# Splitting the second group's operands step by step, and moving the finish of reloaded blocks into the v stage

## The chip, the cores and the metric

The kernel runs on one core of a Trainium2 chip. The metric is device time in microseconds (us). The kernel before takes 2644.31 us, the median of three runs between 2639.09 and 2648.97. A core has five engines that matter here: TensorE (PE, matmuls), VectorE (DVE), ScalarE (ACT), GpSimd (POOL), and SyncE (SP). Each runs its own instructions in order. In this kernel SP's DMA queue carries the weights, and POOL's queue carries the activations, spills and results.

## The reference

One layer of a decoder, for a prompt of 2048 tokens and a sample batch of 8 x 8 tokens, in float32:

```python
z = rms_norm(x, pre_g)
xr, gr, u, v, gs = split(z @ w_in)            # 5 x 1024 columns
xc, new_buf = causal_depthwise_conv(xr, conv_buf, conv_w, conv_b)
r, i = sigmoid(xc . w_r + b_r), sigmoid(xc . w_i + b_i)     # per head
a = exp(-8 r softplus(-lam));  h_t = a_t h_{t-1} + sqrt(1 - a_t^2) i_t xc_t
br = h * silu(gr)
v = rms_norm(gelu(v), sgu_g)
bs = gelu(u) * (tril(w_s) @ v per chunk of 128 + b_s) * silu(gs)
y = x + rms_norm(concat([br, bs]) @ w_out, post_g)
```

The outputs are y for prompt and sample, the last three rows of the convolution, the last h, and the sample's normalised v.

## The kernel before

The prompt is cut into four groups of 512 tokens. Group 0 also carries the 64 sample tokens. Every large product is made of three matmuls on rounded halves: a float32 matrix is split into a high part (hi, made by ACT) and the rest (lo, made by DVE), and hi x hi, hi x lo and lo x hi are added in PSUM. Weights come as 128 x 1024 blocks of 512 KB by SP's queue (`wraw`, L176). ACT makes `wh` (L184), DVE makes `wl` (L192). The pools hold three of each.

Group 0 uses ordinary products (`gm0...`, L363), laid out by a scheduler. Its jobs end with 16 `out` jobs. In these also the beginning of group 1 is done: `stat_load` loads x in a token-major form (`xs`, L613), `stat_sum` squares and sums it on ACT (L621), `stat_rstd` makes the inverse root mean square and spreads it on a diagonal (`xd`, L630, DVE), `stat_spread` multiplies with ones on PE (`nsx`, L635), `stat_take` copies it back (L639). `z_raw` loads x in the form for the products (`xr`, L643), `z_norm` normalises it (L649, DVE).

Groups 1 to 3 use a Strassen-like scheme of seven products (`PROD` = B11, P4, B21, P2, P1, P3, B22) with the operands A11, A22, A12, E, D1, D3, F (`ACTS`). `pre` (L666 to L672, DVE) forms E, D1, D3 and F in place of the blocks of A, `z_hi` (ACT, L678) and `z_lo` (DVE, L683) split them into the tiles R1A, R1E, R1D, R1F that PE reads. (The trace merges A11, A22, A12 under R1A, and D1, D3 under R1D.) These groups run under a schedule by hand: `steps2` is a list of weight blocks with their matmuls, and `at2(step, f, ...)` hangs a piece of other work on a step. Within a step each engine executes: the loads of weights 6 steps ahead, `wh` 3 steps ahead, the hung work, `wl` 3 steps ahead, then the matmuls. So an instruction that waits on ACT or DVE holds up the weight halves of the following steps.

One group has 196 steps. From its first step G: four quads `xg0` to `xg3` of 14 steps (columns xr and gr); the v stage of 28 steps from V = G + 56; four quads `ug` from U = G + 84; and two wide stages of the output product, 28 steps each, from O = G + 140. The convolution, the gates and the scan of a quad (ACT lines L855 to L870, DVE lines L874 to L885) hang on the steps behind it. The end of the v stage's first product, `vn` (ACT, L789, gelu from PSUM) and its squares (`vq`, L910), stands about 12 steps into that stage.

The finish of a group's result y = x + rms_norm(out) needs the sum of squares over all columns, so it is done in the next group. Group 0's 16 blocks of 288 KB are spilled to DRAM and reloaded (`finish0_load`, L595), scaled on DVE (`finish0_scale`, L599), x is added by an accumulating DMA (`finish0_add`, L602), and the result stored (`finish0_store`, L605). Of the later groups' eight blocks of 512 KB, four stay in SBUF and four are spilled and reloaded (`finish_load`, L994); then `finish_scale` (L1000, twice per block), `finish_add` (L1004) and `finish_store` (L1007). `load_gq` (L983) loads a piece of the post-norm gain. All these DMAs but gq are issued on POOL.

Nearly all large tiles (xr, gr, gates, r, i, q, t, vn, u, the reloaded blocks fo, gq, xs) are taken in turn from one pool of 13 buffers of 128 x 2 x 516 floats:

```python
dp = ctx.enter_context(tc.tile_pool(name="dp", bufs=13))
```

A new tile waits until the buffer's last user is through. Where that is a DMA, the instruction waits for its landing. Tiles are assigned to buffers in the order in which the program asks for them.

Of the kernel before, what the change touches and what calls it, by code (L numbers as in the profile page):

```python
# [51 lines left out]
def hybrid_layer(ctx: ExitStack, tc: tile.TileContext, a):  # L52
# [683 lines left out]
    def at2(s, f, *args):  # L736

        tasks[s].append((f, *args))
# [337 lines left out]
    def at(job, f, *args):  # L1076
        plan[job].append((f, *args))
# [26 lines left out]
        t = 60 + 20.5 * n  # L1104
        by_step[next(i for i, x in enumerate(when) if x >= t)].append((make_sums, u))
    for n in range(8):
        at(("out", 8 + n // 4), stat_load, 1, n)
        at(("out", 9 + n // 4), stat_sum, 1, n)
    for f in (stat_rstd, stat_spread, stat_take):
        at(("out", 11), f, 1)  # L1110
    for j in range(8):
        at(("out", 10 + j // 2), z_raw, 1, j)
        at(("out", 12 + j // 3), z_norm, 1, j)

    z_load(0)
    make_identity(nc, ident)
# [30 lines left out]
    zlo = ctx.enter_context(tc.tile_pool(name="zlo", bufs=4, reuse_waits="tile"))  # L1147
    zhi = ctx.enter_context(tc.tile_pool(name="zhi", bufs=4, reuse_waits="tile"))

    for c in ACTS:  # L1150
        for j in range(4):
            if c == "E":
                pre(("R", 1), "D3", j)
            if c in ("E", "D1", "F"):
                pre(("R", 1), c, j)
            z_hi(("R", 1), c, j)
            z_lo(("R", 1), c, j)

    def combine(key, c, j, s):

        at2(s, z_hi, key, c, j)
        at2(s + 1, z_lo, key, c, j)

    for g in range(1, NG):
        G = len(steps2)
        V, U, O, R2 = G + 56, G + 84, G + 140, G + 168
        for n, us in enumerate(XG):
            quad(g, f"xg{n}", us, put_xg(g, 2 * n))  # L1170
            e, k = len(steps2), (g, 2 * n)
            at2(e - 8, gate_weights, *k)
            at2(e - 3, gate_weights_split, *k)
            at2(e, conv_first, *k, 0)
            at2(e + 1, conv_first, *k, 1)
            for m in range(6):
                at2(e + 1 + m // 2, conv_tap, *k, m // 3, 1 + m % 3)
            at2(e + 4, gate_hi, *k)
            at2(e + 5, gate_lo, *k)
            at2(e + 6, act, ("gr", *k), AF.Silu)  # L1180
            late[e + 6].append((gate_mm, *k, 0))
            at2(e + 7, gate_sig, *k, 0)
            late[e + 8].append((gate_mm, *k, 1))
            at2(e + 9, gate_sig, *k, 1)
            at2(e + 10, lru_tanh, *k)
            ts = (11, 11, 12, 13, 14, 18, 20, 21, 22) if n < 3 else (10, 11, 11, 12, 13, 14, 15, 16, 17)
            for t, (f, *args) in zip(ts, ((mul, ("i", *k), ("xc", *k)), (lru_exp, *k), (lru_sq, *k), (lru_mult, *k),
                                          (act, ("t", *k), AF.Sqrt), (mul, ("i", *k), ("t", *k)),
                                          (lru_scan, *k, 0), (lru_scan, *k, 1), (lru_end, *k))):
                at2(e + t, f, *args)  # L1190
        wide(g, "v", "w_v", 0, put_v(g))
        if g == 1:
            for j in range(KT):
                t = 4 + 3 * j // 2 if j < 10 else V + 11 + 2 * (j - 10)
                at2(t, finish0_load, j)
                t = max(t + 3, 9)
                at2(t, finish0_scale, j)
                at2(t + 1, finish0_add, j)
                at2(t + 4, finish0_store, j)
        else:  # L1200
            at2(G - 1, load_gq, g - 1, 1)
            for n in range(4):
                k = (g - 1, (1, 1, 0, 0)[n], (3, 2, 2, 3)[n])
                at2(G + 4 + n, finish_scale, *k)
                at2(G + 5 + n, finish_add, *k)
                at2(G + 10 + n, finish_store, *k)
            at2(G + 8, load_gq, g - 1, 0)
            for n in range(4):
                k = (g - 1, n % 2, n // 2)
                at2(G + 5 + n, finish_load, *k)  # L1210
                at2(G + 11 + n, finish_scale, *k)
                at2(G + 12 + n, finish_add, *k)
                at2(G + 17 + n, finish_store, *k)
        at2(U + 2, norm_v, g)
        at2(U + 3, scale_v, g, 0)
        at2(U + 5, scale_v, g, 1)
        for n, us in enumerate(UG):
            quad(g, f"ug{n}", us, put_ug(g, 2 * n))
            e, k = len(steps2), (g, 2 * n)
            for i in range(2):  # L1220
                late[e - 10 + 2 * i].append((spatial_prod, *k, i))
                at2(e - 9 + 2 * i, spatial_take, *k, i)
            at2(e + 1, act, ("u", *k), AF.Gelu_apprx_tanh)
            at2(e + 2, mul, ("u", *k), ("s", *k))
            at2(e + 3, act, ("gs", *k), AF.Silu)
            at2(e + 4, end_u, *k)
        B, key = O - 14, ("C", g)
        for j in range(4):
            combine(key, "A11", j, B + 3 + j)
            combine(key, "A22", j, (B + 7, B + 7, B + 8, O + 5)[j])  # L1230
            at2((B + 8, B + 10, B + 12, O + 2)[j], pre, key, "D3", j)
            combine(key, "A12", j, (B + 9, B + 11, B + 12, O + 6)[j])
            s = (B + 10, B + 13, O + 1, O + 7)[j]
            at2(s, pre, key, "E", j)
            combine(key, "E", j, s + 1)
            at2(O + 8 + j, pre, key, "D1", j)
            combine(key, "D1", j, O + 9 + j)
            combine(key, "D3", j, O + 13 + j)
            at2(O + 17 + j, pre, key, "F", j)
            combine(key, "F", j, O + 18 + j)  # L1240
        for q in range(2):
            wide(g, f"o{q}", "w_or", q, put_o(g, q))
        at2(len(steps2) + 2, out_rstd, g)
        if g + 1 < NG:
            for n in range(8):
                at2(O + 2 + 3 * n // 2, stat_load, g + 1, n)
                at2(O + 5 + 3 * n // 2, stat_sum, g + 1, n)
            at2(O + 18, stat_rstd, g + 1)
            late[O + 19].append((stat_spread, g + 1))
            at2(O + 20, stat_take, g + 1)  # L1250
            for j in range(8):
                at2(O + 18 + j, z_raw, g + 1, j)
                for i in range(2):
                    at2(O + 22 + 2 * j + i, z_norm, g + 1, j, (i,))
            key = ("R", g + 1)
            for j in range(4):
                combine(key, "A11", j, R2 + 2 + j)
                combine(key, "A22", j, R2 + 8 + j)
                at2(R2 + 10 + j, pre, key, "D3", j)
                combine(key, "A12", j, R2 + 12 + j)  # L1260
                at2(R2 + 14 + j, pre, key, "E", j)
                combine(key, "E", j, R2 + 16 + j)
                at2(R2 + 18 + j, pre, key, "D1", j)
                combine(key, "D1", j, R2 + 19 + j)
                combine(key, "D3", j, R2 + 23 + j)
                at2(R2 + 21 + j, pre, key, "F", j)
                combine(key, "F", j, R2 + 26 + j)
# [97 lines left out]
```

## Time and profile before

| what | value |
|---|---|
| median of 3 runs | 2644.31 us (2639.09 to 2648.97) |
| the profiled execution, its own time | 2642.0 us |
| its span in the trace | 2640.0 us |
| mean granted TensorE clock | 0.981 of full speed |
| PE busy | 2523.5 us (96%) |
| DVE busy | 1767.9 us (67%) |
| ACT busy | 1390.9 us (53%) |
| POOL busy | 339.9 us (13%) |
| bytes by SP's queue | 383.36 MB |
| bytes by POOL's queue | 201.11 MB |

The span of a quad (14 steps) without disturbance is 43.1 us in this trace, that of a v stage 83.2 to 86.2 us. A row of waits gives who waited, at which line, for which engine and tile, then the sum of us, the number of waits and the longest. A row of groups gives line, engine, operation, tiles and shapes, then busy time, mean ns of one, and the idle time ahead of it with what ended it. In a row of DMA issues the last number is the median us from issue to landing. The granted clock is that of PE, 1.00 being full speed.

### The profile page before, as it was taken

The numbers are of one execution on the slowest core, as the hardware profiler recorded it, in microseconds if no ns is written. First come the engines' busy times: TensorE is split into PE (matmuls) and PEld (weight loads), VectorE is DVE, ScalarE is ACT, GpSimd is POOL, SyncE is SP. The second block draws the span as 40 slices with busy tenths as digits, with TensorE's granted clock in tenths as the row PEclk, the third lists the DMA queues.
The fourth block names the chain that finished last, engine by engine and source line by source line (L and its number), as shares of the span: only waits on it lengthen the run. The fifth ranks groups of instructions, "written<-read, shape, count | busy, mean of one in ns | idle before, by whom it ended". The sixth has DMA issues, their size and how long they took to land.

```text
span 2640.0 us, 41631 instructions
## 1 busy us (share of the span) xinstructions
PE 2523.5 (96%) x16710; PEld 2321.1 (88%) x16710; DVE 1767.9 (67%) x2293; ACT 1390.9 (53%) x1778; POOL 339.9 (13%) x492
## 2 busy tenths in 40 slices
PE   7999999899998999999999999999999899999994
PEld 6999789899988998899878898899878898899883
DVE  7885255545457687656888586656788686666855
ACT  5445331123234577645766577645765577555642
POOL 4332023323331200100100200000100200000000
PEclk9999999999998999999999999999999999999997
DMA  6994378865864855756876955556776965555555
GB/s 224 342 342 174 118 262 307 313 247 196 315 235 151 280 183 178 239 180 182 266 260 210 299 192 163 184 180 189 269 238 216 297 191 165 184 183 177 185 190 191
DMA packets 168802, 587.12 MB, mean 222 GB/s; under 512 B 19344, under 2 KB 19904, under 8 KB 168608
## 3 DMA queue, kind: packets, MB, share of 16 engines
q1 hardware_dynamic: 110064, 383.36, 44.3%
q0 software_dynamic: 58544, 201.11, 22.4%
q8 instruction: 130, 2.13, 0.3%
q14 instruction: 64, 0.52, 0.1%
HBM read 494.92 MB, written 89.47 MB: 221 GB/s over the span
## 4 chain that ended last, share of the span: by engine, by line
PE 72%; DMA 10%; DVE 7%; ACT 6%; issue 4%; POOL 1%; SPq 0%; DVEq 0%; ACTq 0%; POOLq 0%
PE gm0out L363 6%; PE gm0v L374 4%; PE gm0gr L363 4%; PE gm0gs L363 3%; PE gm0xr L363 2%; DMA wraw_c_P<-P_c 1%; DMA pB22c<-w_in 1%; PE gm0u L363 1%; PE g L849 1%; PE sp L552 1%; PE w3vd L709 1%; DVE wl_c_B L192 1%; PE w2o1a L709 1%; PE w1o1a L709 1%; PE w2o0a L709 1%
## 5 line engine op out<-in xcount | busy, mean ns | idle before, releaser
L184 ACT ACTIVATE wh_c_P<-wraw_c_P 128x1024 fp32r<-128x1024 f32 x192 | 203.2, 1059 | 277.0 <-DMA wraw_c_P<-P_c 69.3
L192 DVE TENSOR_TENSOR wl_c_P<-wraw_c_P,wh_c_P 128x1024 fp32r<-128x1024 f32 x192 | 234.7, 1223 | 113.4 <-ACT wh_c_P L184 111.5
L192 DVE TENSOR_TENSOR wl_c_B<-wraw_c_B,wh_c_B 128x1024 fp32r<-128x1024 f32 x144 | 175.5, 1222 | 86.9 <-ACT wh_c_B L184 86.8
L184 ACT ACTIVATE wh_c_B<-wraw_c_B 128x1024 fp32r<-128x1024 f32 x144 | 151.9, 1056 | 140.2 <-DMA wraw_c_B<-w_in 44.1
L192 DVE TENSOR_TENSOR wl_w_or_P<-wraw_w_or_P,wh_w_or_P 128x1024 fp32r<-128x1024 f32 x96 | 117.5, 1223 | 50.1 <-ACT wh_w_or_P L184 49.7
L184 ACT ACTIVATE wh_w_or_P<-wraw_w_or_P 128x1024 fp32r<-128x1024 f32 x96 | 101.5, 1057 | 84.6 <-DMA wraw_w_or_P<-P_w_or 20.8
L184 ACT ACTIVATE wh_w_or_B<-wraw_w_or_B 128x1024 fp32r<-128x1024 f32 x72 | 76.1, 1058 | 79.6 <-DMA wraw_w_or_B<-w_or 18.4
L363 PE MATMUL gm0out<-c0l,wh_out 128*128 128x288 f32 x512 | 111.9, 300 | 1.2 <-DVE c0l L158 1.1
L363 PE MATMUL gm0out<-c0h,wh_out 128*128 128x288 f32 x512 | 110.4, 297 | 0.9 <-ACT wh_out L184 0.9
L192 DVE TENSOR_TENSOR wl_w_or_B<-wraw_w_or_B,wh_w_or_B 128x1024 fp32r<-128x1024 f32 x72 | 88.0, 1222 | 34.6 <-ACT wh_w_or_B L184 34.3
L363 PE MATMUL gm0out<-c0h,wl_out 128*128 128x288 f32 x512 | 110.2, 297 | 0.5 <-DVE wl_out L192 0.5
L363 PEld LDWEIGHTS gm0out<-c0l,wh_out 128*128 128x128 f32 x512 | 83.1, 190 | 2.6 <-DVE c0l L158 1.9
L363 PEld LDWEIGHTS gm0out<-c0h,wl_out 128*128 128x128 f32 x512 | 83.1, 190 | 1.2 <-DVE wl_out L192 0.7
L363 PEld LDWEIGHTS gm0out<-c0h,wh_out 128*128 128x128 f32 x512 | 83.0, 189 | 1.2 <-ACT wh_out L184 1.1
L613 POOL DMA_DIRECT2D xs<-xt x24 | 12.8, 536 | 510.5 <-ACT wh_c_P L184 259.1
L192 DVE TENSOR_TENSOR wl_w_v_P<-wraw_w_v_P,wh_w_v_P 128x1024 fp32r<-128x1024 f32 x48 | 58.5, 1222 | 28.2 <-ACT wh_w_v_P L184 28.2
L184 ACT ACTIVATE wh_out<-wraw_out 128x1024 fp32r<-128x1024 f32 x32 | 33.7, 1056 | 81.6 <-PE gm0out L363 53.9
L184 ACT ACTIVATE wh_w_v_P<-wraw_w_v_P 128x1024 fp32r<-128x1024 f32 x48 | 49.9, 1054 | 46.8 <-DMA wraw_w_v_P<-P_w_v 30.1
L192 DVE TENSOR_TENSOR wl_out<-wraw_out,wh_out 128x1024 fp32r<-128x1024 f32 x32 | 41.1, 1286 | 42.9 <-ACT wh_out L184 42.8
L363 PE MATMUL gm0xr<-z0h,wh_xr 128*128 128x288 f32 x256 | 56.5, 302 | 8.1 <-ACT wh_xr L184 5.4
L374 PE MATMUL gm0v<-wl_v,z0h 128*128 128x512 f32 (+1 forms) x160 | 63.5, 397 | 0.0
L374 PE MATMUL gm0v<-wh_v,z0l 128*128 128x512 f32 (+1 forms) x160 | 63.4, 396 | 0.0
(1598 smaller groups left out, 8553.6 us busy)
## 6 DMA issues: line engine op xcount, KB each, us to landing
wraw_c_P<-P_c SPq DMA_DIRECT2D x192, 512.0 KB, 3.9
wraw_c_B<-w_in SPq DMA_DIRECT2D x144, 512.0 KB, 4.2
wraw_w_or_P<-P_w_or SPq DMA_DIRECT2D x96, 512.0 KB, 4.2
wraw_w_or_B<-w_or SPq DMA_DIRECT2D x72, 512.0 KB, 4.0
wraw_w_v_P<-P_w_v SPq DMA_DIRECT2D x48, 512.0 KB, 3.6
wraw_w_v_B<-w_v SPq DMA_DIRECT2D x36, 512.0 KB, 3.3
wraw_out<-w_out SPq DMA_DIRECT2D x32, 512.0 KB, 4.8
xs<-xt POOLq DMA_DIRECT2D x24, 512.0 KB, 6.5
```

Source lines behind the costliest of these rows:

```text
L184: nc.scalar.activation(h[:, sl], raw[:, sl], AF.Copy)
L192: nc.vector.tensor_sub(l[:, sl], raw[:, sl], h[:, sl].bitcast(F32))
L363: nc.tensor.matmul(p[:, :n], w, zz[:, o:o + n], start=(k == 0 and n_pass == 0), stop=(k == KT - 1 and n_pass == 2))
L374: nc.tensor.matmul(p[:n], zz[:, c * P:c * P + n], w, start=(k == 0 and n_pass == 0), stop=(k == KT - 1 and n_pass == 2))
L552: nc.tensor.matmul(p[:, c * P:(c + 1) * P], state["vn", c, h // 4][:, vs], wst[:, h, :], start=True, stop=True)
L613: side.dma_start(x, a[f"xt{g}"][c * P:(c + 1) * P, b * W:(b + 1) * W])
L709: nc.tensor.matmul(bks[b], zz, w, start=(not cont and kk == 0 and n_pass == 0), stop=(kk == HALF - 1 and n_pass == 2), skip_group_check=True)
L849: nc.tensor.matmul(p, ww[:, ws], xx[:, i, :TP], start=n_pass == 0, stop=n_pass == 2)
```

## The change

There are five parts. (1) In group 0's out jobs, the loads and sums of group 1's statistics move from jobs 8 to 10 to jobs 3 to 8, `stat_rstd` to job 9, spread and take to job 10; `z_raw` and `z_norm` move two and one jobs ahead. (2) Before the hand-laid schedule only A11 and A22 of group 1 are split, and D3, E and D1 are formed. A12, E, D1, D3 are split at steps 0 to 8, F is formed at 5 to 8 and split at 8 to 10. (3) `gate_weights` of group 1's first quad is hung three steps later. (4) Group 0's reloaded blocks: the first eight from step 12, two steps apart, the others from V + 3 (before: ten from step 4, six from V + 11). (5) In groups 2 and 3 the kept blocks are two steps apart, and the reloaded ones go, with their gq, from the group's first steps to V + 2 to V + 27.

```diff
     for n in range(8):
-        at(("out", 8 + n // 4), stat_load, 1, n)
-        at(("out", 9 + n // 4), stat_sum, 1, n)
-    for f in (stat_rstd, stat_spread, stat_take):
-        at(("out", 11), f, 1)
+        at(("out", 3 + n // 2), stat_load, 1, n)
+        at(("out", 5 + n // 2), stat_sum, 1, n)
+    at(("out", 9), stat_rstd, 1)
+    at(("out", 10), stat_spread, 1)
+    at(("out", 10), stat_take, 1)
     for j in range(8):
-        at(("out", 10 + j // 2), z_raw, 1, j)
-        at(("out", 12 + j // 3), z_norm, 1, j)
+        at(("out", 8 + j // 2), z_raw, 1, j)
+        at(("out", 11 + j // 3), z_norm, 1, j)
...
-    for c in ACTS:
+    for c in ("A11", "A22"):
         for j in range(4):
-            if c == "E":
-                pre(("R", 1), "D3", j)
-            if c in ("E", "D1", "F"):
-                pre(("R", 1), c, j)
             z_hi(("R", 1), c, j)
             z_lo(("R", 1), c, j)
+    for c in ("D3", "E", "D1"):
+        for j in range(4):
+            pre(("R", 1), c, j)
...
+    for j in range(4):
+        combine(("R", 1), "A12", j, j // 2)
+        combine(("R", 1), "E", j, 2 + j // 2)
+        combine(("R", 1), "D1", j, 4 + j // 2)
+        combine(("R", 1), "D3", j, 6 + j // 2)
+        at2(5 + j, pre, ("R", 1), "F", j)
+        combine(("R", 1), "F", j, 8 + j // 2)
...
-            at2(e - 8, gate_weights, *k)
+            at2(e - 8 if g > 1 or n else e - 5, gate_weights, *k)
...
         if g == 1:
             for j in range(KT):
-                t = 4 + 3 * j // 2 if j < 10 else V + 11 + 2 * (j - 10)
+                t = 12 + 2 * j if j < 8 else V + 3 + 2 * (j - 8)
                 at2(t, finish0_load, j)
-                t = max(t + 3, 9)
+                t += 3
...
-                at2(G + 4 + n, finish_scale, *k)
-                at2(G + 5 + n, finish_add, *k)
-                at2(G + 10 + n, finish_store, *k)
-            at2(G + 8, load_gq, g - 1, 0)
+                t = G + (5, 7, 9, 11)[n]
+                at2(t, finish_scale, *k)
+                at2(t + 1, finish_add, *k)
+                at2(t + 6, finish_store, *k)
+            at2(V + 2, load_gq, g - 1, 0)
             for n in range(4):
                 k = (g - 1, n % 2, n // 2)
-                at2(G + 5 + n, finish_load, *k)
-                at2(G + 11 + n, finish_scale, *k)
-                at2(G + 12 + n, finish_add, *k)
-                at2(G + 17 + n, finish_store, *k)
+                t = V + 9 + 4 * n
+                at2(t - 6, finish_load, *k)
+                at2(t, finish_scale, *k)
+                at2(t + 1, finish_add, *k)
+                at2(t + 6, finish_store, *k)
```

`combine(key, c, j, s)` hangs `z_hi` on step s and `z_lo` on step s + 1.

On DVE, at the start of group 1 and before the change, the order is as follows (a part of the 24 rows between two weight splits):

```order
L192 TENSOR_TENSOR wl_c_0_P_8000<-wraw_c_0_P_7990,wh_c_0_P_7998 128x1024
L683 TENSOR_TENSOR R1A_0_7912<-xr_4_7505,R1A_0_7912 128x512
...
L683 TENSOR_TENSOR R1E_7926<-xr_4_7505,R1E_7926 128x512
...
L683 TENSOR_TENSOR R1D_0_7945<-xr_0_7239,R1D_0_7945 128x512
...
L672 TENSOR_TENSOR xr_4_7505<-xr_4_7505 128x2x256
...
L683 TENSOR_TENSOR R1F_7985<-xr_7_7635,R1F_7985 128x512
L192 TENSOR_TENSOR wl_c_0_P_8031<-wraw_c_0_P_7992,wh_c_0_P_8029 128x1024
```

In the changed kernel the same place reads:

```order
L192 TENSOR_TENSOR wl_c_0_P_7940<-wraw_c_0_P_7926,wh_c_0_P_7934 128x1024
L683 TENSOR_TENSOR R1A_0_7936<-xr_4_7263,R1A_0_7936 128x512
L683 TENSOR_TENSOR R1A_1_7938<-xr_5_7265,R1A_1_7938 128x512
L192 TENSOR_TENSOR wl_c_0_P_7977<-wraw_c_0_P_7928,wh_c_0_P_7969 128x1024
L683 TENSOR_TENSOR R1A_2_7973<-xr_6_7391,R1A_2_7973 128x512
L683 TENSOR_TENSOR R1A_3_7975<-xr_7_7393,R1A_3_7975 128x512
L192 TENSOR_TENSOR wl_c_0_B_8015<-wraw_c_0_B_7930,wh_c_0_B_8005 128x1024
L683 TENSOR_TENSOR R1E_8009<-xr_4_7263,R1E_8009 128x512
L683 TENSOR_TENSOR R1E_8011<-xr_5_7265,R1E_8011 128x512
L192 TENSOR_TENSOR wl_c_0_B_8052<-wraw_c_0_B_7932,wh_c_0_B_8044 128x1024
```

What stood between two weight splits in one piece now stands two by two behind each.

On POOL, in the v stage of group 2, the changed kernel has these rows, where there were none before (the names fo_0_0 and so on are the half and the column quarter of the block; `o` is the spilled copy, `xt` the input):

```order
L994 DMA fo_0_0_15945<-o_0_0_12866 128x2x512 [waits DVE_49,PE_49]
L994 DMA fo_1_0_16045<-o_0_1_13174 128x2x512 [waits DVE_49]
L1004 DMA fo_0_0_15945<-xt 128x2x512 [waits DMASW7_49,DVE_49]
L994 DMA fo_0_1_16142<-o_1_0_13262 128x2x512 [waits DMASW2_49,DVE_49,PE_49]
L1004 DMA fo_1_0_16045<-xt 128x2x512 [waits DMASW3_49,DMASW0_49,DVE_49]
L1007 DMA y<-fo_0_0_15945 128x2x512 [waits DMASW4_49,DMASW1_49]
```

So the first store stands behind the third block's load and the second block's add. And on ACT, at the same place, what follows the tile q of the scan is (`DMASW` are the landings of POOL's DMAs):

```order
L870 ACTIVATE q_6_16140<-r_6_16042 128x2x512 [waits Activation_49]
L184 ACTIVATE wh_w_v_2_P_16160<-wraw_w_v_2_P_16088 128x1024 [waits DMAHW1_49,DVE_49,PE_49]
L789 ACT_TABLE_LOAD [waits DMASW4_49]
L789 ACTIVATE vn_0_16163<-w2va_15881 128x512 [waits DMASW1_49]
L910 ACTIVATE vq_0_0_16165,vss_16162<-vn_0_16163 128x512 [waits Activation_49]
L184 ACTIVATE wh_w_v_3_P_16186<-wraw_w_v_3_P_16111 128x1024 [waits DMAHW2_49,DVE_49,PE_49]
```

Before, the table load and vn stood at the same place and named no DMA; the buffer of vn is now that of fo_0_0.

## The prediction

> **What bounds the kernel now.** I read the page first, then a table of stages, then what TensorE (PE) waited for in the stages that are too long. The page says that PE is busy nearly all the time.
>
> ```profile
> span 2640.0 us, 41631 instructions
> PE 2523.5 (96%) x16710; PEld 2321.1 (88%) x16710; DVE 1767.9 (67%) x2293; ACT 1390.9 (53%) x1778; POOL 339.9 (13%) x492
> ```
>
> So an edit gains only what it takes from the remaining 116.5 us without work on PE, or from stretches at a lower granted clock, and anything that stops PE costs in full. The view by windows, cut at stage borders, shows which stages hold that time. Columns: window, its length, then busy us and count for PE, weight loads, DVE, ACT, POOL; granted clock; DMA share; GB/s. The rows are group 1's quads xg0, xg1, xg2 and its v stage, then group 2's xg0, xg1 and v stage, then group 3's xg0 and xg1.
>
> ```profile
> 826.10:882.60 56.50, 45.60 (x346) 43.21 (x345) 43.16 (x68) 27.29 (x41) 11.64 (x16) 0.88 0.57 164
> 882.60:928.60 46.00, 43.54 (x350) 42.14 (x349) 30.57 (x39) 30.30 (x36) 12.32 (x18) 1.00 0.91 307
> 928.60:971.70 43.10, 42.89 (x351) 41.96 (x350) 33.15 (x42) 31.86 (x37) 0.73 (x1) 1.00 0.54 178
> 1014.70:1100.90 86.20, 84.01 (x350) 66.27 (x349) 61.76 (x68) 57.66 (x71) 11.92 (x18) 0.98 0.73 226
> 1426.50:1470.20 43.70, 41.06 (x337) 40.84 (x336) 30.96 (x47) 19.26 (x26) 10.44 (x12) 0.98 0.95 285
> 1470.20:1519.90 49.70, 46.54 (x350) 44.07 (x349) 30.45 (x39) 29.73 (x36) 9.34 (x10) 0.95 0.88 288
> 1606.50:1690.00 83.50, 82.34 (x350) 65.02 (x349) 58.45 (x63) 58.49 (x72) 0.00 (x0) 1.00 0.56 176
> 2017.70:2062.80 45.10, 41.25 (x338) 41.05 (x337) 31.57 (x47) 19.41 (x26) 11.55 (x14) 0.96 0.95 292
> 2062.80:2109.80 47.00, 44.02 (x351) 42.57 (x350) 29.71 (x39) 29.63 (x35) 8.19 (x10) 1.00 0.89 289
> ```
>
> The undisturbed quad, xg2, takes 43.1 us. The disturbed ones go with a DMA share of 0.88 to 0.95, except the very first, where the DMA is slack (0.57). The view of PE's waits names them: the out stage of group 0 first, then group 1's xg0, group 2's xg0 and xg1, group 3's xg0.
>
> ```profile
> PE nsx L635 <- DVE xd L630: 3.8, 1, 3.8
> PE q1xg0e L695 <- DVE wl_c_P L192: 7.4, 1, 7.4
> PE q1xg0e L695 <- ACT wh_c_P L184: 2.3, 1, 2.3
> PE q2xg0d L695 <- DVE wl_c_B L192: 2.6, 1, 2.6
> PE g L849 <- ACT r L855: 2.4, 1, 2.4
> PE q3xg0d L695 <- DVE wl_c_B L192: 3.8, 1, 3.8
> ```
>
> **The change part by part.** Each term below is set against the profiled execution (2642.0 us around a span of 2640.0).
>
> *Statistics begun sooner.* In ten-microsecond windows the out stage and the start of group 1 look so:
>
> ```profile
> 760.00:770.00 10.00, 8.64 (x63) 8.17 (x62) 3.98 (x11) 7.89 (x12) 2.98 (x3) 1.00 0.41 137
> 770.00:780.00 10.00, 6.25 (x31) 5.00 (x30) 7.72 (x10) 1.28 (x3) 4.15 (x6) 0.83 0.96 354
> 840.00:850.00 10.00, 4.72 (x22) 4.72 (x23) 7.49 (x10) 2.35 (x4) 0.93 (x2) 0.50 0.63 193
> 850.00:860.00 10.00, 10.00 (x78) 9.18 (x78) 6.29 (x15) 3.82 (x6) 0.00 (x0) 0.99 0.35 113
> ```
>
> A full window holds 78 matmuls, 0.128 us each. From 760 to 780 there are 63 + 31 = 94 instead of 156: 62 missing, 7.9 us. The chain is: ACT's sums (L621) wait for the loads of xs, the sum gives rstd, DVE builds xd, and PE's nsx stands in order behind that.
>
> ```profile
> ACT xs L621 <- DMA xs<-xt: 7.2, 3, 5.1
> L635 PE MATMUL nsx<-xd,ones 128*128 128x512 f32 x2 | 2.0, 1106 | 3.8 <-DVE xd L630 3.8
> ```
>
> nsx itself (about 1.1 us of PE time) stays. The change loads xs at out jobs 3 to 6, sums at 5 to 8, and asks for nsx two jobs after the last sum, so the 7.2 us of waiting for loads should lie ahead of it. Gain 7.9 - 1.1, less 0.5 for the two matmul waits that may remain: **-6.3** (range -8 to -4). The eight z_raw loads two jobs sooner, and gate_weights of the first quad three steps later, lie on POOL's queue, where nothing of those jobs waits at its end; both go at nothing (a miss would be one transfer, some 5 us, by the row of o<-o below).
>
> *Group 1's operands split by steps.* Before, all seven operand sets are split ahead of the second group's first steps. DVE does this between two weight splits:
>
> ```profile
> L683 DVE TENSOR_TENSOR R1D<-xr,R1D 128x512 fp32r<-128x512 f32 x8 | 4.9, 682 | 0.0
> L683 DVE TENSOR_TENSOR R1A<-xr,R1A 128x512 fp32r<-128x512 f32 x4 | 3.7, 993 | 0.0
> L683 DVE TENSOR_TENSOR R1F<-xr,R1F 128x512 fp32r<-128x512 f32 x4 | 2.5, 689 | 0.0
> L672 DVE TENSOR_TENSOR xr<-xr 128x512 f32<-128x512 f32 x4 | 2.5, 686 | 0.0
> L683 DVE TENSOR_TENSOR R1E<-xr,R1E 128x512 fp32r<-128x512 f32 x4 | 2.5, 680 | 0.0
> ```
>
> These are 16.1 us in which no weight half is made, and PE stops. Of the stage's 56.5 us, 56.5 - 45.6 = 10.9 are without work, and the 22 matmuls of 840:850 took 4.72 us instead of 22 x 0.128 = 2.8: 1.9 more, at clock 0.50. Together 12.8. The change puts the same instructions between the weight splits, each set shortly ahead of its use. But the sum on DVE does not shrink: through the first eight steps (8 of 24 matmuls at about 2.8 us, 22.5 us) it has eight weight splits of 1.22 us (9.8), 13.6 of the 16.1, and about 3 for the output statistics (dgo): 26.4. About 4 us must still come out as waits of PE, most likely at nsCo, which stands behind dgo. Gain 12.8 - 4.3: **-8.5** (range -12 to -3).
>
> *Finish of group 0's blocks.* Ten of the 16 blocks were asked for from step 4, now eight from step 12, two steps apart. xg0 is freed of their loads, which is in the term above; they now all fall on xg1 and the start of xg2, beside gate work. There ACT's gate tiles take over the buffers of blocks 0 to 4 and wait for their stores. xg1 lost 46.0 - 43.1 = 2.9; with three such waits of about 2 us each I take 6.4: **+3.5** (0 to +7). The other eight move from V+11 to V+3 on; that belongs to the next part.
>
> *Finish of groups 1 and 2.* The four kept blocks are spread, and the four reloaded ones leave the start of the next group. It lost, for group 2, 2.6 idle and about 1 at clock 0.98 in xg0, and 49.7 - 43.1 = 6.6 in xg1: 10.2. For group 3: 3.9 idle, 1.6 at clock 0.96, and 47.0 - 43.1 = 3.9: 9.4. Leaving 1.5 to 2 for the kept blocks: **-8.7 and -7.5** (each -10 to -5).
>
> The reloaded blocks land in the v stage, with DMA share 0.56 and POOL idle before: bandwidth is there. But they come into a shared pool of 13 buffers, and by the order of instructions the first output tile of the v stage, vn, takes the buffer of the first reloaded block, whose store to y is issued just ahead of it. So ACT has a new wait for a store's landing, and behind it in ACT's queue stand the weight halves (wh) of all later steps. At this place before, ACT and DVE ran:
>
> ```profile
> 1644.74 1.06 ACT L870 ACTIVATE q<-r 128x1024 f32<-128x1024 f32 x1
> 1646.77 1.28 ACT L789 ACT_TABLE_LOAD   x1
> 1648.07 0.60 ACT L789 ACTIVATE vn<-w2va 128x512 f32<-128x512 f32 x1
> 1645.84 1.23 DVE L874 SCALAR_TENSOR_TENSOR t<-q,t 128x1024 f32<-128x1024 f32 x1 [2.52 <-ACT q L870]
> 1646.98 1.22 DVE L192 TENSOR_TENSOR wl_w_v_P<-wraw_w_v_P,wh_w_v_P 128x1024 fp32r<-128x1024 f32 x1
> ```
>
> and the new instructions have these prices elsewhere:
>
> ```profile
> L1004 POOL DMA_DIRECT2D fo<-xt x4 | 4.9, 1223 | 12.5 <-DVE fo L1000 4.9 <-DMA fo<-xt 2.9 <-DVE xr L791 2.4
> L1007 POOL DMA_DIRECT2D y<-fo x4 | 3.0, 742 | 12.2 <-DMA fo<-xt 11.2 <-issue 1.0
> L1000 DVE SCALAR_TENSOR_TENSOR fo<-fo,ors,gq 128x512 f32<-128x512 f32 x8 | 5.6, 748 | 1.7 <-DMA gq<-post_g 1.7
> o<-o POOLq DMA_DIRECT2D x4, 512.0 KB, 5.2
> y<-fo POOLq DMA_DIRECT2D x16, 288.0 KB, 7.0
> y<-fo POOLq DMA_DIRECT2D x8, 512.0 KB, 11.3
> ```
>
> On POOL the store stands behind the load of a block whose buffer is freed by t (DVE L874, ends 1647.07), and behind the add of the second block, which waits for two scalings (L1000) that stand behind wl: 1648.20 + 2 x 0.75 = 1649.7. Add issued by 1650.9, store by 1651.7. Landing, counted from 1650.9: 5.2 us in a lightly loaded stage, 11.3 in the saturated start of a group; I take 6.1, near the first, since the share here is 0.56. So it lands at 1657.0, the table load follows (1.28), vn starts at 1658.3 instead of 1648.07: 10.2 late. PE has about 1 us of lead there (an estimate: it waits for no weight half at that place now), and a stop of this length costs 1.9 of slow clock as at 840: 11.1, say **+11 in each of the two v stages** (+6 to +16.5 by the two landings). The Trainium skill, "DMA: Bandwidth & Descriptors", section "Anatomy of one DMA — SWDGE (gpsimd) path", fits such a transfer as 2.0 us plus its bytes over 436 GB/s. By it a 512 KB store lands in an estimated 3.2 us, the wait is 2.9 us shorter in each group and the total 5.8 less; the trace's lightest row of this size has 5.2, so I keep the rows.
>
> Group 1's v stage has the same chain with 288 KB: after q ends, t 1.2, a load's issue 0.5, the store's 0.7, 7.0 less the issue to land, table 1.3: vn about 10 after q instead of the 2.3 that the rows above show, but POOL's queue is ahead by one block there, so I take 8 late; with lead and clock 8.9, less the 2.7 (86.2 - 83.5) that the old places of the six blocks cost: **+6** (0 to +9).
>
> The sum: -6.3 - 8.5 + 3.5 + 6 - 8.7 - 7.5 + 22 = **+0.5**, so 2642.5 for an execution like the profiled one. That one lies 2.3 below the median of the three runs (2644.3), which makes 2644.8: **2645 us**.
>
> **Rivals.** *Faster: the store is never in vn's way by much.* If POOL runs ahead of vn (its instructions have nothing else to do there) and the store lands some 3 us after its issue, each v stage pays 3, group 1's 2: -31.0 + 3.5 + 2 + 6 = -19.5, about **2625**. For it: POOL idle, the DMA half idle. Against: the add cannot issue before 1649.7, already later than vn's old start, and the lightest row is 5.2.
>
> *Slower: the landings in the v stage are the saturated ones.* Load, add and store of three blocks follow each other within 5 us on one queue; at 11.3 to land, vn waits 15 and each v stage loses 16.5, group 1's 9, xg1 6: -31.0 + 6 + 9 + 33 = +17, **2661**. It decides from a wait of about 14 us at vn. For it: the row of 11.3, and 7.0 even for 288 KB. Against: those ran with DMA shares of 0.88 and more.
>
> *The split does not do what it says.* If DVE's 26.4 us lie so that the weight halves are as late as now, only at other steps, the second term gives 3 instead of 8.5: **2651**. For it: the sum on DVE; against: no single block of 16 us is left.
>
> **How the numbers follow.** My forecast 0.45 (its own range 2634 to 2656), the faster rival 0.27, the slower one 0.20, the last 0.08. A difference under 0.5% (13.2 us) can hardly be told from none in this kernel. The forecast and the last rival lie within that: faster 0.27, same 0.53, slower 0.20. The range reaches half into both outer cases: 2621 to 2662.
>
> **What would show it.** Right: no wait of PE at nsx; wl of q1xg0e no longer waited for 7 us, small waits at nsCo instead; xg0 and xg1 of groups 2 and 3 close to 41 and 43 us; a wait of ACT at L789 for the DMA y<-fo of about 10 us in the v stages of groups 2 and 3, with PE stopped at w2v and w3v right after, and v stages of about 94 us. Wrong: v stages near 84 us, which is the faster rival; waits of 14 and more at vn, the slower; or group 1's xg0 still above 53 us.

## The result, and the profile after

The changed kernel takes 2658.06 us (median of 6 runs, 2653.08 to 2660.78), the kernel before 2642.48 us in the same comparison: a ratio of 1.0058, 95% interval [1.0044, 1.0073]. It is slower by 15.6 us. The profiled execution took 2657.97 us, its span is 2656.3 us.

The lengths of the stages, from the first matmul of one to the first of the next in the view of PE's instructions by tile, show where it went (us):

| stage | before | after | difference | forecast |
|---|---|---|---|---|
| out stage of group 0 | 216.9 | 222.3 | +5.4 | -6.3 |
| group 1, xg0 | 56.5 | 50.0 | -6.5 | -8.5 |
| group 1, xg1 | 46.0 | 46.9 | +0.9 | +3.5 |
| group 1, v stage | 86.2 | 89.9 | +3.7 | +6 |
| group 2, xg0 and xg1 | 93.4 | 85.7 | -7.7 | -8.7 |
| group 3, xg0 and xg1 | 92.1 | 85.0 | -7.1 | -7.5 |
| group 2, v stage | 83.5 | 97.9 | +14.4 | +11 |
| group 3, v stage | 83.2 | 97.6 | +14.4 | +11 |
| all others together | | | -1.2 | 0 |
| span | 2640.0 | 2656.3 | +16.3 | +0.5 |

Each length is from one trace. In the kernels below that leave a stage as it was, group 1's xg0 takes 56.3 to 56.5 us and the v stages of groups 2 and 3 take 83.1 to 83.9, trace by trace. The out stage varies more: with the old statistics it takes 210.7 to 216.9 us in seven traces, and the kernel before has the longest.

Two rows carry the miss: the out stage, which has the wrong sign, and the v stages, larger than forecast. The view by windows of the changed kernel, cut at its own borders, has these rows: group 1's xg0, group 2's xg0, xg1 and v stage, group 3's v stage (columns as in the prediction).

```profile
830.90:880.90 50.00, 45.36 (x346) 42.89 (x346) 40.55 (x64) 27.69 (x41) 4.30 (x5) 0.93 0.47 155
1429.90:1470.60 40.70, 39.96 (x337) 39.55 (x336) 28.50 (x43) 18.87 (x26) 7.31 (x8) 1.00 0.84 243
1470.60:1515.60 45.00, 43.35 (x350) 42.02 (x349) 27.18 (x35) 29.95 (x36) 1.64 (x3) 1.00 0.69 224
1601.80:1699.70 97.90, 85.74 (x351) 66.25 (x350) 62.58 (x70) 58.14 (x72) 10.74 (x12) 0.95 0.70 220
2197.30:2294.90 97.60, 85.70 (x351) 66.36 (x350) 62.74 (x70) 58.39 (x72) 11.93 (x14) 0.95 0.72 221
```

In group 2's v stage PE had nothing to do for 97.90 - 85.74 = 12.2 us, against 83.50 - 82.34 = 1.2 before; that is 11.0 of the 14.4. The other 3.4 are longer busy time for the same matmuls (85.74 instead of 82.34, granted clock 0.95 instead of 1.00); 2.5 of it lie right behind the stop, as the last section shows. What PE and ACT waited for in the changed kernel, in the view of waits:

```profile
PE w2vb L709 <- ACT wh_w_v_P L184: 8.7, 1, 8.7
PE w3vb L709 <- ACT wh_w_v_P L184: 7.4, 1, 7.4
PE gm0out L363 <- ACT wh_out L184: 5.5, 3, 2.8
PE nsCo L289 <- DVE dgo L287: 3.7, 1, 3.7
ACT L789 <- DMA y<-fo: 10.4, 1, 10.4
ACT vn L789 <- DMA y<-fo: 9.1, 1, 9.1
ACT xs L621 <- DMA xs<-xt: 37.3, 5, 11.1
```

The waits of the start (wl_c_P 7.4 at q1xg0e, xd 3.8 at nsx) are gone, and nsCo's small wait is there as expected. New are the stops in the two v stages and, not expected, the wait for wh_out. The out stage before and after, by windows, and ACT's wait for xs in it before:

```profile
609.20:826.10 216.90, 210.59 (x1550) 207.86 (x1550) 115.20 (x141) 62.11 (x82) 66.31 (x92) 0.99 0.69 242
608.60:830.90 222.30, 214.20 (x1550) 210.99 (x1550) 112.82 (x141) 61.80 (x82) 75.56 (x92) 0.98 0.66 237
ACT xs L621 <- DMA xs<-xt: 18.0, 5, 10.6
```

PE's idle time there grew only from 6.3 to 8.1 us; the other 3.6 are longer busy time for the same matmuls, with the granted clock down to 0.72 in its lowest 10 us. In time order, around the store that vn waits for (ACT, then POOL):

```profile
1639.87 1.06 ACT L870 ACTIVATE q<-r 128x1024 f32<-128x1024 f32 x1
1652.32 1.28 ACT L789 ACT_TABLE_LOAD   x1 [10.44 <-DMA y<-fo]
1653.61 0.60 ACT L789 ACTIVATE vn<-w2va 128x512 f32<-128x512 f32 x1
1642.83 0.74 POOL L994 DMA_DIRECT2D fo<-o  x1 [10.78 <-issue]
1645.09 1.19 POOL L1004 DMA_DIRECT2D fo<-xt  x1 [1.51 <-DVE fo L1000]
1645.84 1.18 POOL L1007 DMA_DIRECT2D y<-fo  x1
```

From the end of q, the prediction had the store issued at 1650.9 - 1645.8 = 5.1 us and landed at 11.2; here it is issued at 1645.84 - 1640.93 = 4.9 and landed at 1652.32 - 1640.93 = 11.4.

### The profile page after: what moved, and what is told of

Read it like the earlier page. It is cut to its first block, busy times and chain, and to the rows that moved or that the text cites. A ratio compares the mean times of both kernels' runs of the same rounds, so it can differ in the third digit from the quotient of the medians.

```text
span 2656.3 us, 41635 instructions
## 1 busy us (share of the span) xinstructions
PE 2528.5 (95%) x16710; PEld 2322.7 (87%) x16710; DVE 1763.9 (66%) x2293; ACT 1389.9 (52%) x1778; POOL 351.0 (13%) x492
## 4 chain that ended last, share of the span: by engine, by line
PE 71%; DMA 10%; DVE 7%; ACT 6%; issue 5%; POOL 1%; SPq 0%; ACTq 0%; DVEq 0%; POOLq 0%
PE gm0out L363 6%; PE gm0v L374 4%; PE gm0gr L363 4%; PE gm0xr L363 2%; PE gm0gs L363 2%; PE gm0u L363 2%; DMA wraw_w_v_P<-P_w_v 1%; DMA pB22c<-w_in 1%; DMA wraw_c_P<-P_c 1%; PE g L849 1%; DVE wl_c_B L192 1%; PE sp L552 1%; DMA y<-fo 1%; DMA wraw_c_B<-w_in 1%; PE w1o1a L709 1%
## 5 line engine op out<-in xcount | busy, mean ns | idle before, releaser
L363 PE MATMUL gm0xr<-z0h,wh_xr 128*128 128x288 f32 x256 | 56.9, 304 | 8.3 <-ACT wh_xr L184 5.4
```

The lines of the kernel that those rows point to most:

```text
L363: nc.tensor.matmul(p[:, :n], w, zz[:, o:o + n], start=(k == 0 and n_pass == 0), stop=(k == KT - 1 and n_pass == 2))
```

## The experiments

A remark on sizes: the kernel before took 2638.6 to 2642.1 us (medians) in the comparisons below, which ran on several chips; so ratios with their intervals are compared, and stages within a trace. One per mille is 2.6 us.

### The parts alone

Three kernels are the one before with one part each. First the statistics:

```diff
-        at(("out", 8 + n // 4), stat_load, 1, n)
-        at(("out", 9 + n // 4), stat_sum, 1, n)
...
+        at(("out", 3 + n // 2), stat_load, 1, n)
+        at(("out", 5 + n // 2), stat_sum, 1, n)
```

with the rest of part 1 (`stat_rstd`, spread, take, `z_raw`, `z_norm`).

> The kernel before with the first part alone (statistics begun sooner). Theory: the loads of xs now fall into a stretch where the DMA is full, ACT's sums wait for them and hold up the weight halves wh_out behind them; the out stage of group 0 takes 222 us instead of 217 and the whole is 4 to 6 us slower than before, with PE waiting for wh_out 5 us in all and no longer for nsx. Rival: the loss before group 1 in the changed kernel comes from another part (the schedule around the split); then this kernel loses nothing in the out stage and is about 6 us faster, the nsx wait being gone.

Measured: 1.0027 [1.0010, 1.0043], 2646.0 us. The out stage takes 219.8 us, PE no longer waits at nsx, and:

```profile
PE gm0out L363 <- ACT wh_out L184: 4.5, 3, 3.1
PE gm0out L363 <- DVE wl_out L192: 2.7, 5, 0.7
ACT xs L621 <- DMA xs<-xt: 36.4, 6, 10.5
```

So part 1 is a loss by itself, of about 7 us (0.27%).

Then the split together with the new places of group 0's blocks:

```diff
+        combine(("R", 1), "A12", j, j // 2)
+        combine(("R", 1), "E", j, 2 + j // 2)
...
-                t = 4 + 3 * j // 2 if j < 10 else V + 11 + 2 * (j - 10)
+                t = 12 + 2 * j if j < 8 else V + 3 + 2 * (j - 8)
```

> The kernel before with the split by steps and the new places of group 0's blocks (parts 2, 3 and 4; the split needs the later places, since the blocks' scaling uses what is computed in the first steps). Theory: group 1's first quad 50 us instead of 56.5, its second 47 instead of 46, its v stage 90 instead of 86: in sum 2 us faster, with a wait of PE for dgo of some 4 us. Rival: without the earlier statistics the split is no gain (A11 is late as well), the first quad stays above 54 us and the whole is slower by 3 or more.

Measured: 0.9985 [0.9971, 1.0000], 2635.5 us; xg0 49.8, xg1 50.0, v stage 90.2. In xg1 ACT waited 6.4 us for a store of group 0 (i, L855). The rival, that the split needs the earlier statistics, falls: the first quad is as short as in the changed kernel.

And part 5 alone:

```diff
...
-                at2(G + 11 + n, finish_scale, *k)
-                at2(G + 12 + n, finish_add, *k)
-                at2(G + 17 + n, finish_store, *k)
+                t = V + 9 + 4 * n
+                at2(t - 6, finish_load, *k)
+                at2(t, finish_scale, *k)
...
```

> The kernel before with the fifth part alone (finish of groups 1 and 2 spread and moved into the v stage). Theory: vn waits for the store of the first reloaded block, 9 to 10.5 us in ACT; v stages of groups 2 and 3 take 97 to 98 us instead of 83.4, the first two quads give back 7 each: +14 us. Rival: the long v stages come from the other parts (a shifted rhythm of POOL's queue); then the v stages stay below 90 and the whole is faster by 5 or more.

Measured: 1.0045 [1.0029, 1.0061], 2648.4 us; v stages of 97.6 and 97.2 us, first two quads 84.5 (before 93.4) and 84.7 (92.1).

```profile
ACT L789 <- DMA y<-fo: 10.3, 1, 10.3
ACT vn L789 <- DMA y<-fo: 9.3, 1, 9.3
```

The wait comes with part 5 and needs no other. The three ratios add up to 1.0027 + 0.9985 + 1.0045 - 2 = 1.0057, the whole change had 1.0058. Each ratio is known to about 0.0015, so an agreement this close is in part chance; there is at least no sign that the parts touch each other.

Of the middle one, the new places of group 0's blocks were also run alone (the last two lines of its diff):

> The kernel before with part 4 alone (new places of group 0's blocks). Theory: without their loads and scalings in the first steps nothing changes there (DVE's 16 us of operands still stand in one piece), so the first quad stays at 56 us; the second takes 47 to 50 instead of 46, the v stage 90 instead of 86: 4 to 7 us slower than before. Rival (the blocks' loads in the first steps were what delayed that quad): the first quad falls below 53.

Measured: 1.0015 [1.0004, 1.0025]; xg0 56.9, xg1 46.1, v stage 90.9. It costs 4 us; of group 1's stages the v stage is longer, by 4.7, and vn waits 3.4 us there for a store. The quad xg1 did not lengthen, and ACT has no wait for a store in it. With the split as well, ACT waits for such a store in every trace with these places, 2.5 to 6.4 us, but xg1 takes 44.4 to 50.0, so the 47 to 50 that I expected are not the rule. That the shorter xg0 brings the stores nearer to their buffers' next users would explain these waits; it was not tested. The split with part 3 is thus worth 1.0015 - 0.9985 = 0.0030, about 8 us, and xg0 is 7.1 us shorter (56.9 and 49.8).

### The wait at vn

The changed kernel with two numbers changed, so that the reloaded blocks and their gq come six steps later:

```diff
-            at2(V + 2, load_gq, g - 1, 0)
+            at2(V + 8, load_gq, g - 1, 0)
...
-                t = V + 9 + 4 * n
+                t = V + 15 + 4 * n
```

> The changed kernel with the four reloaded blocks of groups 1 and 2 six steps later in the v stage (first scaling at V + 15 instead of V + 9, the load of gq at V + 8), so that vn asks for its buffer before they do and takes one that no DMA holds. Same work, same transfers, same stage. Theory (the wait is for the buffer alone): no wait of ACT at vn, v stages of groups 2 and 3 at 84 to 87 us, 22 to 28 us faster than the changed kernel, some 10 faster than before. Rival (the stage is too full for the transfers and scalings as such): v stages stay above 92 us, less than 12 us won.

Measured: 0.9990 [0.9976, 1.0005], 2637.8 us, against 1.0058 for the change: 18 us won. ACT has no wait for y<-fo in the v stages of groups 2 and 3 any more, and they take 88.0 and 87.5 us. Group 2's v stage by windows:

```profile
1592.10:1680.10 88.00, 83.96 (x351) 64.64 (x350) 61.25 (x68) 57.37 (x71) 7.80 (x9) 1.00 0.72 222
```

PE still has 4.0 us without work there, against 1.2 before, and 1.6 us more busy. So of the 14.4 us about 10 were the wait for the buffer. About 4.5 remain with the added work at these steps: PE's waits there are five of at most 0.9 us, most of them for wl. They are no fixed price of that work: spaced otherwise (the respaced kernel below) the same stages are only 2.9 and 2.4 longer than before. I had expected 84 to 87, so the gain fell at the low side, below the 22 us that I gave.

The second test of the same wait moved only the stores:

```diff
-                at2(t + 6, finish_store, *k)
+                at2(t + 4, finish_store, *k)
```

> The changed kernel with the stores of the four reloaded blocks two steps sooner (t + 4 instead of t + 6), all else in place. On POOL the first store now stands ahead of the second block's add instead of behind it, so it is issued about 2.3 us sooner (at 1643.6 instead of 1645.8 on the clock of the changed kernel's trace); vn takes the same buffer. Theory (vn waits for this store's landing): ACT's wait at L789 falls by 2 to 3 us in group 2 (10.4 to about 8) and in group 3 (9.1 to about 7), and the two v stages shorten by as much, to about 95 us. Rival (what is waited for is the stretch of transfers as a whole, load, add and store): the wait stays at 9 to 10.

Measured: 1.0058 [1.0035, 1.0081], no gain. In its trace the store is issued 3.7 us after q begins (1639.88 - 1636.19) instead of 6.0 (1645.84 - 1639.87), so 2.3 sooner, but:

```profile
ACT L789 <- DMA y<-fo: 9.3, 1, 9.3
ACT vn L789 <- DMA y<-fo: 7.8, 1, 7.8
```

The waits fell by 1.1 and 1.3, half of it, and the v stages stayed at 97.6 and 98.0. The landing took 1647.52 - 1639.88 = 7.6 us instead of 1652.32 - 1645.84 = 6.5. In both traces the store was issued 0.7 us behind another 512 KB transfer (now a load, there an add), and the DMA share is near 1 while it is under way (1.02 from 1642 to 1644 here, 1.01 from 1646 to 1648 there); which of this makes the 1.1 us was not settled. Neither statement was right. The wait follows this store, though by less than its issue moved. What was won at vn was lost again in the stage:

```profile
1598.30:1695.90 97.60, 87.23 (x350) 68.03 (x349) 64.15 (x71) 58.72 (x72) 10.80 (x12) 0.93 0.73 221
```

PE is idle for 10.4 us instead of 12.2, but busy for 87.2 instead of 85.7, at a granted clock of 0.93 instead of 0.95.

### The out stage

Back to the old statistics, with the later blocks kept:

```diff
-        at(("out", 3 + n // 2), stat_load, 1, n)
-        at(("out", 5 + n // 2), stat_sum, 1, n)
...
+        at(("out", 8 + n // 4), stat_load, 1, n)
+        at(("out", 9 + n // 4), stat_sum, 1, n)
...
```

(the rest of part 1 goes back too).

> The changed kernel with the reloaded blocks six steps later in the v stage, and with the statistics of group 1 put back where they were before (part 1 undone). Theory (part 1 costs by itself, whatever stands behind it): the out stage of group 0 takes 212 to 217 us instead of 220 to 222, the whole 5 to 8 us less than with the later blocks alone, some 6 to 8 below before. Rival (the earlier statistics are needed by the split): the out stage is shorter, but group 1's first quad longer than 52 us, and nothing is won.

Measured: 0.9976 [0.9966, 0.9987], 2634.3 us. The out stage takes 214.5 us, the first quad 50.1. It is below the 0.9990 of the kernel with the earlier statistics by 0.0014, about 4 us and less than the 5 to 8 expected, and the intervals touch.

Whether the loads or the sums do it was to be told by sums that stand two jobs later in the program:

```diff
-        at(("out", 5 + n // 2), stat_sum, 1, n)
-    at(("out", 9), stat_rstd, 1)
+        at(("out", 7 + n // 3), stat_sum, 1, n)
+    at(("out", 10), stat_rstd, 1)
```

> The changed kernel with the reloaded blocks six steps later, with the loads of the statistics as in the change (out jobs 3 to 6) but their sums on ACT at jobs 7 to 9 instead of 5 to 8, and rstd at job 10 instead of 9. Theory (the sums stand ahead of wh_out in ACT's queue and wait for loads that are still under way): ACT's wait for xs falls below 15 us, PE waits for wh_out less than 1.5 us, the out stage takes 213 us or less instead of 220 to 222, 6 to 8 us better than with the later blocks alone. Rival (the full DMA itself delays the weights of w_out): ACT no longer waits for xs but PE still waits 4 us and more in the out stage, which stays at 219 or above.

Measured: 0.9999 [0.9989, 1.0009]; ACT waits 36.9 us for xs, the out stage takes 222.3 us. This told nothing: group 0 is laid out by the scheduler, and it put the sums at the very rows of ACT's order where they had been, between the same weight halves. To hold them back they must depend on something late. So in a later kernel (which starts from the respaced one below) their bias is a zero made from the output of job 6 or 8:

```diff
+        if j in (6, 8):
+            state["zb", j] = zb = mp.tile([P, 1], F32, tag="zb", name=f"zb{j}")
+            nc.vector.tensor_scalar(zb, o[:, :1], 0.0, None, op0=ALU.mult)
...
-        nc.scalar.activation(x, x, AF.Square, accum_out=state["xss", g][:, c, b:b + 1])
+        zb = 0.0 if g > 1 else state["zb", 6 if n < 4 else 8]
+        nc.scalar.activation(x, x, AF.Square, bias=zb, accum_out=state["xss", g][:, c, b:b + 1])
```

with the loads at jobs 3 to 6, as in the change, and the sums hung on jobs 6 and 8.

> The respaced kernel, with the statistics' loads early as in the change, but with the sums on ACT really held back: their bias is a zero made from the output of job 6 (first four) and job 8 (last four), so that the scheduler can't put them ahead of it. The order on ACT now has the sums two to three jobs behind where the change had them. Theory (sums that wait in ACT's queue for loads are what costs, not the loads): ACT's wait for xs below 10 us (37 in the change), PE's wait for wh_out below 1.5, the out stage 211 to 214 us (220 to 222 with the change's statistics, 212 to 217 with the old). Rival (the full DMA delays the weights): the out stage at 218 or above.

Measured: 0.9951 [0.9935, 0.9967], the same as the respaced kernel with the old statistics (0.9958 [0.9945, 0.9972]). The out stage takes 212.4 us. ACT's wait for xs is gone from the list, and of PE's waits in the out stage remain:

```profile
PE gm0out L363 <- DVE wl_out L192: 1.6, 1, 1.6
PE nsx L639 <- DVE xd L634: 1.3, 1, 1.3
PE gm0out L363 <- DVE c0l L158: 0.8, 1, 0.8
```

The same loads at the same jobs, and no wait for wh_out: the waits for wh_out come from the sums in front of it in ACT's queue. But the early loads may not be free. In the kernel with both last edits (below), whose sums are held too, the out stage takes 218.3 us. There DVE waits for other loads, those of w_or, which stand on POOL's queue behind those of xs; these waits lie in front of wl_out in DVE's order, are 37.6 us in all against 17.3 before, and one of them reaches PE. Two rows from that kernel, then one from the kernel before:

```profile
PE gm0out L363 <- DVE wl_out L192: 4.5, 1, 4.5
DVE pB11w_or L241 <- DMA pB12w_or<-w_or: 37.6, 5, 11.7
DVE pB11w_or L241 <- DMA pB12w_or<-w_or: 17.3, 5, 6.2
```

In the 212.4 us trace DVE waits 31.2 us in the same way, and PE 1.6. So the rival, the full DMA, seems to have a part, 1.6 and 4.5 us of PE's time in the two traces; no run tests that alone. Out stages over all profiles: 219.8 to 222.7 us in the five with early sums, 210.7 to 216.9 in the seven with the old statistics, 212.4 and 218.3 in the two with held sums.

### Towards a better version

From the kernel with old statistics and later blocks, the blocks' steps were chosen anew, by the order of instructions, so that ACT waits for few young stores:

```diff
-                t = 12 + 2 * j if j < 8 else V + 3 + 2 * (j - 8)
+                t = 20 + 3 * j if j < 6 else V + 7 + 2 * (j - 6)
...
-            at2(V + 8, load_gq, g - 1, 0)
+            at2(V + 6, load_gq, g - 1, 0)
...
-                t = V + 15 + 4 * n
+                t = V + 13 + 5 * n
```

> As the one with the old statistics and the later reloaded blocks, but with the reloaded blocks five steps apart from V + 13 on, and group 0's blocks at other steps: six from step 20 on, three apart, and ten from V + 7 on, two apart, so that by the order of instructions ACT waits for hardly any of their stores. Theory: group 1's second quad at 44 us or less instead of 46 to 50, its v stage at 87 instead of 90, the v stages of groups 2 and 3 at 86 instead of 88; 5 to 9 us better than without the new steps, 12 to 16 below before. Rival (the v stage is full and the work only changes places): group 1's v stage above 89 us, less than 3 us won.

Measured: 0.9958 [0.9945, 0.9972], 2625.8 us. In groups 1 to 3 no wait of ACT for a y store is left in the trace. xg1 takes 43.0 us, the three v stages 87.2, 86.4 and 85.6. As the theory had it, except that xg2 and xg3 together take 88.4 instead of 86, where part of the blocks now lies.

Last, the wait at nsCo, the one stop of more than 1 us left in group 1's first quad:

```diff
-    late[4].append((norm_a, "o"))
-    late[7].append((norm_b, "o"))
+    late[11].append((norm_a, "o"))
+    late[15].append((norm_b, "o"))
```

> The respaced kernel, with the norm of group 0's result (dgo, nsCo, rsBo) hung at steps 11 and 15 of group 1 instead of 4 and 7; its first use is now at step 23. Theory (DVE has more to do than fits in the first eight steps, and nsCo's wait is where it shows): the 3.7 us wait of PE at nsCo goes, the first quad takes 42 to 45 us instead of 50, the whole 4 to 8 us less than the respaced one. Rival (the weight halves are late as well): PE waits for wl in the same steps and the quad stays at 48 or more.

Measured: 0.9932 [0.9911, 0.9953], 2622.0 us, the lowest ratio of all and 18 us below the kernel before. Its interval touches that of the respaced kernel. The first two quads by windows:

```profile
818.00:858.80 40.80, 40.80 (x343) 39.97 (x342) 37.37 (x59) 27.95 (x41) 4.46 (x5) 1.00 0.57 188
858.80:905.20 46.40, 44.48 (x355) 42.60 (x354) 29.50 (x41) 29.64 (x35) 2.57 (x4) 1.00 0.58 184
```

The first has no idle time on PE and the full clock. It went from 50.0 to 40.8; the second gained 3.4 us, part of it the matmuls of the norm themselves, which moved there (343 and 355 matmuls). Net 5.8 by these two quads, within the 4 to 8 that were expected.

Both of the last edits together:

> Both edits, the later norm and the sums held back. Theory: they lie in different stages and add up: out stage 211 to 214 us, first quad 42 to 45 us, 5 to 10 us below the respaced kernel, about 20 below before. Rival: the norm's DVE work meets the gate work of the first quad at steps 14 on, and the second quad gives half of it back.

Measured: 0.9937 [0.9921, 0.9953]. They do not add up: it is no better than the later norm alone, its second quad takes 46.6 us (46.4 there), and its out stage 218.3 instead of the 211 to 214 expected. In the end the held sums win nothing over the old statistics here.

## Why the prediction was right and wrong, point by point

**The new wait at vn: right in place, chain and size.** Read from the order of instructions and priced by rows of before, it was to make vn 10.2 us late; ACT waited 10.4 and 9.1. The landing was nearer to 5.2 than to 11.3, as I had taken it: 6.5 from issue. The reason that I gave, a mean share of 0.56 over the stage, says less than it seems: around this landing the share was near 1 (1.01 and 1.10 in the two 2 us windows from 1646 to 1650), as in the stages where 11.3 was read, and the four such stores of this stage took 7.3 us in the median. That the size came out is partly luck. Nor is 5.2 the lightest row of this size on POOL's queue, as I had written; the kernel before has also

```profile
P_w_v<-pB12w_v POOLq DMA_DIRECT2D x4, 512.0 KB, 3.3
o<-D1o POOLq DMA_DIRECT2D x1, 512.0 KB, 3.2
```

The Trainium skill, "DMA: Bandwidth & Descriptors", section "Anatomy of one DMA — SWDGE (gpsimd) path", by whose fit such a transfer takes an estimated 3.2 us, agrees with these lightest rows; the landing here took twice that.

**The cost of the v stage: mis-sized.** The term was "vn 10.2 late, less 1 of lead, plus 1.9 of slow clock": 11. It measured 14.4. In group 2 the stop of PE was 8.7 (the lead was 1.7: a wait of 10.4 on ACT became 8.7 on PE), close to the 9.2 of the forecast. PE's other waits for weight halves grew by 2.3, a term that I had put at nothing because the DMA is half idle and POOL wholly. Busy time grew by 3.4, of which 2.5 are the slow clock behind the stop, where I had 1.9. The kernel with later blocks shows a cost of the work without any wait at vn: the scalings, loads and stores cost about 4.5 us in this stage, and 2.4 to 2.9 with other steps. That the added work makes DVE's and ACT's weight halves late is my reading of these small waits (0.3 to 1.1 us; one of 0.9 at w2vd stood in before already); no run takes the scalings out alone.

**The statistics: wrong in sign.** The step that failed is "the 7.2 us of waiting for loads should lie ahead of" nsx. They do lie ahead of it, but in ACT's queue, in front of the weight halves of w_out. Nor was 7.2 the whole: it is the wait in 760 to 780 alone, and over the out stage ACT waited 18.0 us for xs before already. Now it waits 37.3, and 5.5 of PE's time go to wh_out, beside the slow clock. I looked at who waits for the sum, and not at what stands behind the sum on its own engine. Instead of -6.3 the out stage changed by +5.4, and by more against the shorter out stages of the other kernels with the old statistics. The run with part 1 alone (0.27% slower) shows that part 1 costs this, and the runs with the sums held show that the waits for wh_out come from the sums. In those runs DVE waits longer instead, and PE stops for 1.6 and 4.5 us at wl_out.

**Group 1's first quad: mechanism right, size near.** Forecast -8.5, measured -6.5. The forecast wait at nsCo came with 3.7 us where I had put 4, and the last experiments show that it, with its slow clock, was worth the rest of the way to 40.8 us, though 3.4 us of that came back in the second quad.

**Group 0's blocks and the starts of groups 2 and 3: right within 3 us each.** Forecast +3.5, +6, -8.7, -7.5, measured +0.9, +3.7, -7.7, -7.1. For the first I had counted three waits; one, of 3.7 us, showed. In group 1's v stage I had put vn 8 late; ACT waited 3.2 there.

**The forecast as a whole.** The likeliest case was 2645 us with its own range up to 2656; measured were 2658, beyond that range and inside the wide one of 2621 to 2662. That the wide range holds it confirms little: it reaches there for the slower rival's sake. The time lies at the slower rival's 2661, but not by that rival's mechanism: its waits of 14 us and more at vn did not occur. It is the sum of the statistics' sign (11.7 us) and of the under-sized v stages (6.8), less 2.7 that the other stages together went better than forecast. (The last rival's sum, 0.5 + 5.5 on 2644.3, gives 2650.3, not 2651.)

## What to carry to other kernels

A change that moves loads and stores into a quiet stage also moves tiles into a pool that other engines share: look in the order of instructions at who gets their buffers next, for a store that must land first is a wait on a compute engine, and everything behind it in that engine's order waits too. Here the blocks six steps later in the same stage won back 18 us. Likewise, when a reduction is asked for sooner, ask what stands behind it on its engine while its data is still on the way; and where a scheduler decides the order, moving a line in the program may move nothing, so look at the order before drawing a conclusion.

## What the runs showed of the hardware that was not expected

After the stop in group 2's v stage the slow clock lasted: in the view by windows of the changed kernel

```profile
1640.00:1645.00 5.00, 5.00 (x23) 4.03 (x22) 3.69 (x4) 1.88 (x2) 0.74 (x1) 1.00 0.36 113
1655.00:1660.00 5.00, 3.58 (x8) 2.49 (x9) 1.68 (x2) 4.94 (x7) 0.00 (x0) 0.50 0.30 98
1660.00:1665.00 5.00, 5.00 (x20) 3.84 (x19) 4.96 (x7) 2.47 (x3) 0.73 (x1) 0.87 0.46 170
```

a matmul of 512 columns takes 5.00 / 23 = 0.22 us ahead of the stop and 3.58 / 8 = 0.45 behind it, and the 28 matmuls of the two windows behind it took 8.58 us instead of 6.1: 2.5 us more, beyond the stop itself. The Trainium skill, "TensorE: Matmul & The Clock Gate", Part 1, has half rate after an idle window of about 3.4 us, and full rate only after as long a busy one; half rate over 3.4 us of work would be an estimated loss of 1.7 us. The trace agrees on the rate (clock 0.50, matmuls of twice the time); its loss of 2.5 us is larger than that estimate.

And a store issued sooner does not land sooner by as much: issued 2.3 us earlier, it took 7.6 us to land instead of 6.5, with the DMA share near 1 in both traces.
